# A QKV projection: x transposed by VectorE in 32x32 blocks instead of by TensorE, float32r operands instead of bf16, w in column chunks

## The chip, the cores and the metric

The kernel runs on one core of one Trainium2 chip. The metric is the device time of that core in microseconds (us). Lower is better. Times are medians of a few executions. The profile describes one execution, and its span is some 1 to 2 us shorter than the time of the same execution.

## The reference

```python
x: (16, 512, 768) float32, w_qkv: (768, 2304) float32     # standard normal
qkv = np.matmul(x, w_qkv)
return np.stack([q, k, v], axis=0)                         # q, k, v: the three 768-column parts
```

Seen as one matrix product it is 8192 x 768 times 768 x 2304. With 128 rows of x to a tile there are 64 tiles. In both kernels a matmul contracts over the partitions, 128 at a time (the 128*128 in the groups of instructions below), so 768 gives six steps, and x is handed to TensorE transposed: 128 values of the contraction index on the partitions, 128 rows along the free axis. A tile takes 24 matmuls with 512 columns of w and 6 matmuls with 256 columns.

## The kernel before

x arrives in its own layout, ScalarE rounds it to bf16, and TensorE transposes it in six 128x128 pieces (matmuls against an identity). Those pieces go to PSUM, and VectorE or ScalarE copies them back to SBUF. The transposes of the next tile are woven between the matmuls of the present one. w is loaded in six row blocks of 128 full rows.

```python
w_bf = wb_pool.tile([P, KT, N3], bf16)
# ... pools: x 2 buffers, xT 3, opsum 7 banks, o 3
for ko in range(KT):                                   # w: 128 partitions, whole rows
    w_scr = w_pool.tile([P, N3], fp32)
    nc.gpsimd.dma_start(w_scr[:], w_qkv[bass.ts(ko, P), :])
    nc.vector.tensor_copy(out=w_bf[:, ko, :], in_=w_scr[:])
# ... emit_tps: one PE transpose; after the sixth, a copy PSUM -> xT
for mi in range(MT):
    # ... load x of tile mi+1, round it to bf16 on ScalarE
    for noff, nsz in n_offs:                           # 512, 512, 512, 512, 256
        ops = opsum_pool.tile([P, 512], fp32, tag="o")
        for ko in range(KT):
            nc.tensor.matmul(ops[:, :nsz], xT[:, ko, :], w_bf[:, ko, noff:noff + nsz],
                             start=(ko == 0), stop=(ko == KT - 1))
            if have_next and ko < 2 and tps_cnt < KT:
                emit_tps(nx_mb, nxT, tps_cnt, use_scalar=(nmi % 2 == 0))
                tps_cnt += 1
        nc.vector.tensor_copy(out=o_sb[:, noff:noff + nsz], in_=ops[:, :nsz])
    # ... three stores, one each to q, k, v
```

## Time and profile before

| | before |
|---|---|
| time, median (lowest to highest) | 419.2 us (419.08 to 419.31) |
| span of the profiled execution | 418.5 us |
| mean granted TensorE clock | 1.00 |
| TensorE busy | 95% |

From the page of the kernel before: busy time of each engine, then TensorE's busy share and its granted clock in tenths over 40 equal slices (9 stands for 90% or more), and the shares of the chain of waits that ended last.

```profile
PE 397.3 (95%) x2260; PEld 210.9 (50%) x2304; DVE 224.6 (54%) x358; ACT 77.7 (19%) x97; POOL 4.0 (1%) x12
...
PE   0589999999999999999999999999999999999996
...
PEclk9999999999999999999999999999999999999999
...
PE 92%; DMA 5%; issue 1%; POOL 1%; DVE 1%; POOLq 0%
```

TensorE bounds this kernel. After the third slice (about 31 us) it never pauses, at full clock, and the chain is TensorE nearly from end to end.

Groups of instructions of the kernel before, with the shapes kept apart. The columns are: line, engine, operation, output and input, count; then busy us and mean ns of one; then the engine's idle time before them and what ended it.

```profile
L113 PE MATMUL ops<-w_bf,nxT 128*128 128x512 bf16 x1468 | 353.4, 380 | 1.4
L113 PEld LDWEIGHTS <-nxT 128*128 128x128 bf16 x1890 | 177.5, 98 | 168.2 <-DVE nxT L88 0.7 <-issue 0.3
L123 DVE COPY o_sb<-ops 128x512 f32<-128x512 f32 x256 | 176.5, 691 | 171.3 <-PE ops L113 171.1
L75 PE MATMUL tps<-id_sb,nx_mb 128*128 128x128 bf16 x378 | 81.9, 223 | 5.5 <-ACT nxT L86 4.5
```

A matmul's "mean ns" is not the spacing of two matmuls: one of 512 columns is listed with 380 ns, yet in the stream they start 0.216 us apart (0.109 at 256 columns, 0.055 to 0.056 for a transpose). The cost is the spacing of their starts: 24 x 0.216 + 6 x 0.109 + 6 x 0.0555 = 6.17 us, the period of a tile seen below. (Some matmul records are missing: 2304 matmuls run, and the page lists 2260.) The transposes take the stream of TensorE for 64 x 6 x 0.055 = 21 us. That is what the change wants to save.

Pieces of the chain of waits of the kernel before, in order of time: start, length, what.

```profile
4.39 22.29 DMA w_scr<-in_w_qkv_dram
...
28.11 8.26 PE ops L113 x41
...
42.11 3.03 PE ops L113 x17
48.28 3.03 PE ops L113 x17
```

The same piece of work comes back every 6.17 us: one tile. 64 x 6.17 = 395 us, and the last matmul ends near 414.8, so all of the start-up is worth 19.9 us of lost TensorE time. The rest, 3.7 us, is the tail.

Stretches of the kernel before: the stretch and its length, busy us of each engine (instructions), granted clock, DMA share, GB/s.

```profile
core 0: us, PE busy (x) PEld busy (x) DVE busy (x) ACT busy (x) POOL busy (x), PEclk, DMA share, GB/s
5.00:10.00 5.00, 0.48 (x5) 0.22 (x3) 0.98 (x1) 1.17 (x2) 0.00 (x0) 1.00 1.01 417
10.00:20.00 10.00, 5.04 (x26) 2.77 (x27) 3.79 (x5) 2.76 (x4) 0.00 (x0) 1.00 1.01 422
```

The loads of the start run at 420 GB/s (417 and 422 in the two stretches).

### The profile page before, as it was taken

The page shows a single profiled execution, that of the slowest core. Times are in us where ns is not written, and L with a number is a line of the kernel's source. Part 1 is how long each engine was busy: PE and PEld are TensorE (multiplying, and loading weights), DVE is VectorE, ACT ScalarE, POOL GpSimd, SP SyncE. Part 2 cuts the span into 40 slices and gives each one's busy share as a digit, 9 for nine tenths or more (in the row PEclk, how much of TensorE's full clock was granted, in tenths as well). Part 3 has the DMA queues.
Part 4 walks back from the last instruction along what each step waited for, and adds up shares of the span by engine and source line. Part 5 has one row for each costly group of instructions (what it writes and reads, how often), then busy time and mean ns, then how long its engine had stood idle before and what let it go on. Part 6 is the DMA issues. An engine that isn't in the chain of part 4 may idle for free.

```text
span 418.5 us, 5827 instructions
## 1 busy us (share of the span) xinstructions
PE 397.3 (95%) x2260; PEld 210.9 (50%) x2304; DVE 224.6 (54%) x358; ACT 77.7 (19%) x97; POOL 4.0 (1%) x12
## 2 busy tenths in 40 slices
PE   0589999999999999999999999999999999999996
PEld 0245555555555555555555555555555555555553
DVE  1456555555555455555555555545555555555554
ACT  3210221221122122022112112212212221221200
POOL 3000000000000000000000000000000000000000
PEclk9999999999999999999999999999999999999999
DMA  8968777778877767877777787787777767778444
GB/s 323 423 258 314 236 257 261 223 272 261 286 219 261 268 226 283 269 246 252 256 241 258 259 285 233 256 262 231 279 263 254 248 253 245 254 267 283 197 184 194
DMA packets 37756, 108.13 MB, mean 258 GB/s; under 512 B 4192, under 2 KB 4192, under 8 KB 36960
## 3 DMA queue, kind: packets, MB, share of 16 engines
q1 hardware_dynamic: 36864, 100.68, 69.7%
q0 software_dynamic: 864, 7.08, 4.1%
q8 instruction: 18, 0.29, 0.3%
q14 instruction: 10, 0.08, 0.1%
HBM read 32.24 MB, written 75.50 MB: 257 GB/s over the span
## 4 chain that ended last, share of the span: by engine, by line
PE 92%; DMA 5%; issue 1%; POOL 1%; DVE 1%; POOLq 0%
PE ops L113 86%; PE tps L75 6%; DMA w_scr<-in_w_qkv_dram 5%; POOL w_scr L66 1%; DVE w_bf L67 0%; DVE o_sb L123 0%; POOLq L151 0%; POOL id_sb masks.py:199 0%; POOL id_sb masks.py:197 0%; POOLq masks.py:199 0%; POOLq L140 0%
## 5 line engine op out<-in xcount | busy, mean ns | idle before, releaser
L113 PE MATMUL ops<-w_bf,nxT 128*128 128x512 bf16 (+1 forms) x1846 | 385.5, 358 | 1.4
L123 DVE COPY o_sb<-ops 128x512 f32<-128x512 f32 (+1 forms) x320 | 201.1, 638 | 171.3 <-PE ops L113 171.1
L113 PEld LDWEIGHTS <-nxT 128*128 128x128 bf16 x1890 | 177.5, 98 | 168.2 <-DVE nxT L88 0.7
L75 PE MATMUL tps<-id_sb,nx_mb 128*128 128x128 bf16 x378 | 81.9, 223 | 5.5 <-ACT nxT L86 4.5
L104 ACT ACTIVATE nx_mb<-nx_m 128x768 bf16<-128x768 f32 x63 | 52.9, 839 | 152.7 <-issue 135.6
L86 ACT ACTIVATE nxT<-tps 128x768 bf16<-128x768 bf16 x31 | 25.2, 811 | 167.9 <-PE tps L75 167.9
L75 PEld LDWEIGHTS <-nx_mb 128*128 128x128 bf16 x378 | 37.4, 100 | 20.9 <-ACT nx_mb L104 4.4
L88 DVE COPY nxT<-tps 128x768 bf16<-128x768 bf16 x32 | 17.8, 557 | 2.2 <-PE tps L75 2.2
L67 DVE CAST w_bf<-w_scr 128x2304 bf16<-128x2304 f32 x6 | 8.2, 1358 | 17.2 <-DMA w_scr<-in_w_qkv_dram 17.2
L113 PE MATMUL ops<-w_bf,xT 128*128 128x512 bf16 (+1 forms) x30 | 9.4, 435 | 6.0 <-DVE w_bf L67 6.0
L113 PEld LDWEIGHTS <-xT 128*128 128x128 bf16 x30 | 3.4, 116 | 9.9 <-ACT xT L86 5.2
L75 PE MATMUL tps<-id_sb,x_mb 128*128 128x128 bf16 x6 | 0.8, 310 | 4.7 <-ACT x_mb L62 4.7
L66 POOL DMA_DIRECT2D w_scr<-in_w_qkv_dram x6 | 3.3, 556 | 0.3 <-issue 0.3
L75 PEld LDWEIGHTS <-x_mb 128*128 128x128 bf16 x6 | 0.6, 138 | 4.7 <-ACT x_mb L62 4.7
L62 ACT ACT_TABLE_LOAD x1 | 1.3, 1283 | 0.7 <-PEq L140 0.7
L62 ACT ACTIVATE x_mb<-x_m 128x768 bf16<-128x768 f32 x1 | 0.8, 842 | 1.7 <-DMA x_m<-in_x_dram 1.7
L86 ACT ACTIVATE xT<-tps 128x768 bf16<-128x768 bf16 x1 | 0.8, 792 | 0.0
masks.py:199 POOL TENSOR_SCALAR_AFFINE_SELECT id_sb<-id_sb 128x128 bf16<-128x128 bf16 x1 | 0.3, 307 | 0.1
masks.py:197 POOL MEMSET id_sb<- 128x128 bf16 x1 | 0.2, 205 | 0.3 <-POOLq L140 0.3
L140 POOL MEMSET const-bfloat16-1.0<- 128x1 bf16 x1 | 0.1, 103 | 0.0
L140 POOL MEMSET const-uint8-127<- 128x1 uint8 x1 | 0.1, 103 | 0.0
L140 POOL MEMSET const-float32-0.0<- 128x1 f32 x1 | 0.1, 100 | 0.2 <-issue 0.2
(1 smaller groups left out, 0.1 us busy)
## 6 DMA issues: line engine op xcount, KB each, us to landing
out_dram<-o_sb SPq DMA_DIRECT2D x192, 384.0 KB, 3.6
nx_m<-in_x_dram SPq DMA_DIRECT2D x63, 384.0 KB, 3.6
w_scr<-in_w_qkv_dram POOLq DMA_DIRECT2D x6, 1152.0 KB, 14.8
x_m<-in_x_dram SPq DMA_DIRECT2D x1, 384.0 KB, 3.0
```

What stands on the lines that cost most here:

```text
L62: nc.scalar.activation(x_mb0[:], x_m0[:], mybir.ActivationFunctionType.Identity)
L66: nc.gpsimd.dma_start(w_scr[:], w_qkv[bass.ts(ko, P), :])
L67: nc.vector.tensor_copy(out=w_bf[:, ko, :], in_=w_scr[:])
L75: nc.tensor.matmul(tps[:, bass.ts(ko, P)], xb_tile[:, bass.ts(ko, P)], id_sb[:], is_transpose=True, start=(ko == 0), stop=(ko == KT - 1),)
L86: nc.scalar.activation(xT_view[:], tps[:], mybir.ActivationFunctionType.Identity)
L88: nc.vector.tensor_copy(out=xT_view[:], in_=tps[:])
L104: nc.scalar.activation(nx_mb[:], nx_m[:], mybir.ActivationFunctionType.Identity)
L113: nc.tensor.matmul(ops[:, :nsz], xT[:, ko, :], w_bf[:, ko, noff:noff + nsz], start=(ko == 0), stop=(ko == KT - 1),)
L123: nc.vector.tensor_copy(out=o_sb[:, noff:noff + nsz], in_=ops[:, :nsz])
L140: nc = _bacc.Bacc("TRN2", target_bir_lowering=False, num_devices=1)
```

## The change

The intent is to take the transposes off TensorE. x is loaded so that each 32-partition group holds one quarter of the contraction index (192 of 768 columns). A 32x32 block transpose on VectorE then yields the layout that the matmuls read, ScalarE writes it again as float32r (fp32r in the listings; called a rounding below), and TensorE runs the product matmuls alone. w is loaded in the matching order, in column chunks (256, then four of 512), so that the first five tiles can start chunk by chunk. ScalarE takes two of the five PSUM evictions of a tile from VectorE. The diff, cut to its core:

```diff
+    mm_dt = mybir.dt.float32r
+    n_offs = [(0, 256)] + [(256 + 512 * i, 512) for i in range(4)]
     # ... pools: x 2 (of four tiles each), xf 3, xT 7, ps 8 banks, o 6
-    for ko in range(KT):
-        w_scr = w_pool.tile([P, N3], fp32)
-        nc.gpsimd.dma_start(w_scr[:], w_qkv[bass.ts(ko, P), :])
-        nc.vector.tensor_copy(out=w_bf[:, ko, :], in_=w_scr[:])
+    def load_w(c):
+        off, sz = n_offs[c]
+        st = ws_pool.tile([P, KT, 512], fp32, name="wst")
+        for i in range(4):
+            nc.scalar.dma_start(
+                st[i * G:(i + 1) * G, :, :sz],
+                w_qkv[i * KC:(i + 1) * KC, off:off + sz].rearrange("(j a) n -> a j n", a=G),
+            )
+        for j in range(0, KT, 2):
+            nc.vector.tensor_copy(out=w_sb[c][:, j:j + 2, :], in_=st[:, j:j + 2, :sz])
+    def load_x(mi, count):
+        t = x_pool.tile([P, 4, 4, KC], fp32, name="xin")
+        rows = x_flat[mi * P:(mi + count) * P, :].rearrange("(g b) k -> b g k", b=G)
+        for i in range(4):
+            dst = t[i * G:(i + 1) * G, :count].rearrange("p t g k -> p (t g) k")
+            nc.sync.dma_start(dst, rows[:, :, i * KC:(i + 1) * KC])
-    # ... emit_tps: TensorE transposes and the copies of their PSUM tile
+    def prep(mi):
+        t, n = xs.pop(mi)
+        xf = xb_pool.tile([P, KT, P], fp32, name="xf")
+        nc.vector.transpose(xf.rearrange("p j (g b) -> p g j b", b=G),
+                            t[:, n].rearrange("p g (j a) -> p g j a", a=G))
+        xt = xT_pool.tile([P, KT, P], mm_dt, name="xt")
+        nc.scalar.activation(xt[:], xf[:], copy)
+        xT[mi] = xt
+    # ... mm: six matmuls of one tile and chunk, then the eviction on VectorE or ScalarE
+    # ... first phase: w chunks 0 to 4, in each the tiles 0 to 4
+    for mi in range(FIRST, MT):
+        if loaded - mi <= 3 and loaded < MT:
+            n = min(4, MT - loaded)
+            load_x(loaded, n)
+            loaded += n
+        if mi + 1 < MT:
+            prep(mi + 1)
+        o_sb = o_pool.tile([P, N3], fp32, name="o")
+        order = range(5) if mi < MT - 1 else (1, 2, 3, 4, 0)
+        for c in order:
+            mm(mi, c, o_sb, c % 2 == 0)
+        store(mi, o_sb)
```

More of the change, by code (lines that the diff above doesn't have):

```diff
@@ L4 @@
 import concourse.tile as tile
-from concourse import bass_utils, mybir
-from concourse.masks import make_identity
+from concourse import mybir
 from concourse._compat import with_exitstack
@@ L19 @@
     P = 128
+    G = 32
     B, T, H = x.shape
@@ L23 @@
     N3 = w_qkv.shape[1]
-    assert N3 == 3 * H
-    assert K % P == 0 and M % P == 0
     KT = K // P
+    KC = K // 4
     MT = M // P
+    fp32 = mybir.dt.float32
+    mm_dt = mybir.dt.float32r
+    copy = mybir.ActivationFunctionType.Identity
     x_flat = x.rearrange("b t h -> (b t) h")
     out_flat = out.rearrange("s b t h -> s (b t) h")
-    n_offs = []
-    o = 0
-    while o < N3:
-        sz = min(512, N3 - o)
-        n_offs.append((o, sz))
-        o += sz
-    bf16 = mybir.dt.bfloat16
@@ L42 @@
-    fp32 = mybir.dt.float32
-    id_pool = ctx.enter_context(tc.tile_pool(name="id", bufs=1))
-    id_sb = id_pool.tile([P, P], bf16)
-    make_identity(nc, id_sb)
-    w_pool = ctx.enter_context(tc.tile_pool(name="w", bufs=6))
+    n_offs = [(0, 256)] + [(256 + 512 * i, 512) for i in range(4)]
+    ws_pool = ctx.enter_context(tc.tile_pool(name="ws", bufs=2))
     wb_pool = ctx.enter_context(tc.tile_pool(name="wb", bufs=1))
-    w_bf = wb_pool.tile([P, KT, N3], bf16)
     x_pool = ctx.enter_context(tc.tile_pool(name="x", bufs=2))
-    xb_pool = ctx.enter_context(tc.tile_pool(name="xb", bufs=2))
@@ L54 @@
-    xT_pool = ctx.enter_context(tc.tile_pool(name="xT", bufs=3))
-    tpsum_pool = ctx.enter_context(tc.tile_pool(name="tpsum", bufs=1, space=bass.MemoryType.PSUM))
-    opsum_pool = ctx.enter_context(tc.tile_pool(name="opsum", bufs=7, space=bass.MemoryType.PSUM))
-    o_pool = ctx.enter_context(tc.tile_pool(name="o", bufs=3))
-    x_m0 = x_pool.tile([P, K], fp32, tag="x")
-    nc.sync.dma_start(x_m0[:], x_flat[bass.ts(0, P), :])
-    x_mb0 = xb_pool.tile([P, K], bf16, tag="xb")
-    nc.scalar.activation(x_mb0[:], x_m0[:], mybir.ActivationFunctionType.Identity)
@@ L64 @@
-    for ko in range(KT):
-        w_scr = w_pool.tile([P, N3], fp32)
-        nc.gpsimd.dma_start(w_scr[:], w_qkv[bass.ts(ko, P), :])
-        nc.vector.tensor_copy(out=w_bf[:, ko, :], in_=w_scr[:])
-    tps_state = {}
-    def emit_tps(xb_tile, xT_tile, ko, use_scalar):
-        if ko == 0:
-            tps_state['t'] = tpsum_pool.tile([P, KT * P], bf16, tag="t", name="tps")
-        tps = tps_state['t']
-        nc.tensor.matmul(
-            tps[:, bass.ts(ko, P)],
-            xb_tile[:, bass.ts(ko, P)],
-            id_sb[:],
-            is_transpose=True,
-            start=(ko == 0),
-            stop=(ko == KT - 1),
-        )
-        if ko == KT - 1:
-            xT_view = xT_tile.rearrange("p k m -> p (k m)")
-            if use_scalar:
-                nc.scalar.activation(xT_view[:], tps[:], mybir.ActivationFunctionType.Identity)
-            else:
-                nc.vector.tensor_copy(out=xT_view[:], in_=tps[:])
@@ L90 @@
-    xT_tiles = {}
-    xT0 = xT_pool.tile([P, KT, P], bf16, tag="xt")
-    xT_tiles[0] = xT0
-    for ko in range(KT):
-        emit_tps(x_mb0, xT0, ko, use_scalar=True)
-    for mi in range(MT):
-        xT = xT_tiles.pop(mi)
-        nmi = mi + 1
-        have_next = nmi < MT
-        if have_next:
-            nx_m = x_pool.tile([P, K], fp32, tag="x")
-            nc.sync.dma_start(nx_m[:], x_flat[bass.ts(nmi, P), :])
-            nx_mb = xb_pool.tile([P, K], bf16, tag="xb")
-            nc.scalar.activation(nx_mb[:], nx_m[:], mybir.ActivationFunctionType.Identity)
-            nxT = xT_pool.tile([P, KT, P], bf16, tag="xt")
-            xT_tiles[nmi] = nxT
-        tps_cnt = 0
-        o_sb = o_pool.tile([P, N3], fp32)
-        for noff, nsz in n_offs:
-            ops = opsum_pool.tile([P, 512], fp32, tag="o")
-            for ko in range(KT):
-                nc.tensor.matmul(
-                    ops[:, :nsz],
-                    xT[:, ko, :],
-                    w_bf[:, ko, noff:noff + nsz],
-                    start=(ko == 0),
-                    stop=(ko == KT - 1),
-                )
-                if have_next and ko < 2 and tps_cnt < KT:
-                    emit_tps(nx_mb, nxT, tps_cnt, use_scalar=(nmi % 2 == 0))
-                    tps_cnt += 1
-            nc.vector.tensor_copy(out=o_sb[:, noff:noff + nsz], in_=ops[:, :nsz])
@@ new lines @@
+    xb_pool = ctx.enter_context(tc.tile_pool(name="xb", bufs=3))
+    xT_pool = ctx.enter_context(tc.tile_pool(name="xT", bufs=7))
+    ps_pool = ctx.enter_context(tc.tile_pool(name="ps", bufs=8, space=bass.MemoryType.PSUM))
+    o_pool = ctx.enter_context(tc.tile_pool(name="o", bufs=6))
+    w_sb = [wb_pool.tile([P, KT, sz], mm_dt, name=f"w{c}") for c, (_, sz) in enumerate(n_offs)]
+    def load_w(c):
[8 more added lines that the diff above has]
+            nc.vector.tensor_copy(out=w_sb[c][:, j:j + 2, :], in_=st[:, j:j + 2, :sz])
@@ new lines @@
+    xs = {}
+    def load_x(mi, count):
[4 more added lines that the diff above has]
+            nc.sync.dma_start(dst, rows[:, :, i * KC:(i + 1) * KC])
+        for n in range(count):
+            xs[mi + n] = (t, n)
+    xT = {}
+    def prep(mi):
+        t, n = xs.pop(mi)
+        xf = xb_pool.tile([P, KT, P], fp32, name="xf")
+        nc.vector.transpose(
+            xf.rearrange("p j (g b) -> p g j b", b=G),
+            t[:, n].rearrange("p g (j a) -> p g j a", a=G),
+        )
+        xt = xT_pool.tile([P, KT, P], mm_dt, name="xt")
+        nc.scalar.activation(xt[:], xf[:], copy)
+        xT[mi] = xt
@@ L124, with mm, store @@
+    def mm(mi, c, o_sb, evac):
+        off, sz = n_offs[c]
+        ps = ps_pool.tile([P, 512], fp32, name="ps")
+        for j in range(KT):
+            nc.tensor.matmul(ps[:, :sz], xT[mi][:, j, :], w_sb[c][:, j, :], start=(j == 0), stop=(j == KT - 1))
+        if evac:
+            nc.vector.tensor_copy(out=o_sb[:, off:off + sz], in_=ps[:, :sz])
+        else:
+            nc.scalar.activation(o_sb[:, off:off + sz], ps[:, :sz], copy)
+    def store(mi, o_sb, parts=3):
         for s in range(3):
@@ L125 @@
             nc.sync.dma_start(out_flat[s, bass.ts(mi, P), :], o_sb[:, bass.ts(s, H)])
+    FIRST = 5
+    load_x(0, 1)
+    load_w(0)
+    load_x(1, 4)
+    prep(0)
+    for c in range(1, 5):
+        load_w(c)
+    for mi in range(1, FIRST):
+        prep(mi)
+    load_x(FIRST, 4)
+    loaded = FIRST + 4
+    o_first = [o_pool.tile([P, N3], fp32, name="o") for _ in range(FIRST)]
+    for c in range(5):
+        for mi in range(FIRST):
+            mm(mi, c, o_first[mi], (mi + c) % 2 == 0)
+            if c == 4:
+                store(mi, o_first[mi])
@@ L129 @@
+    prep(FIRST)
+    for mi in range(FIRST, MT):
[10 more added lines that the diff above has]
+        store(mi, o_sb)
 _INS = ['x', 'w_qkv']
```

## The prediction

> **What bounds the kernel now.** TensorE. The page's first part shows it 95% busy, and the chain of waits puts 92% of the span on it (86% product matmuls, 6% transposes). The timeline shows matmuls starting every 0.216 us (512 columns), about 0.11 us (256) and 0.055 us (128, the transposes). One 128-row tile is therefore 24 x 0.216 + 6 x 0.11 + 6 x 0.055 = 6.17 us, which is the period seen between pieces of the chain; 64 tiles make 395 us. The last matmul ends near 414 us, so start-up costs about 19 us of TensorE time (it runs without gaps only from 28 us, when the last row block of w has been cast). The tail is 4 us. VectorE is 54% busy, ScalarE 19%, DMA about 0.76 in the steady part (stretches table), 1.01 at 420 GB/s during the first 20 us.
>
> **What the change does.**
> 1. Removes the 384 PE transposes and their PSUM copies: 64 x 6 x 0.055 = -21 us on the critical path.
> 2. Product matmuls stay 1920 in number and the same in shape, but float32r, and each loads its own weights. [...] Loads took 98 ns in the trace with bf16; if slower they can still hide under 0.216 us, less surely under 0.11 us. No run here shows either yet. This is the largest risk: an unhidden 98 ns load would add 1920 x 0.098 = 188 us.
> 3. VectorE gains 64 transposes of 128x768 fp32. From the two evictions (512: 691 ns, 256: 424 ns) I estimate 0.96 us each. It loses two of five evictions to ScalarE: per tile 0.96 + 0.42 + 2 x 0.69 = 2.8 us of a 5.84 us period. ScalarE: 0.84 + 2 x about 0.6 = 2.0 us. Neither binds. Bursts of four transposes (about 4 us) fit into eight PSUM banks (over 8 us of TensorE work).
> 4. x comes in 768-byte runs instead of 3 KB. DMA work now is about 4.7 us per tile, a quarter of it x; even 1.5 times for x gives 5.3 us, under 5.84 but close.
> 5. Start-up. w in column chunks should let TensorE start early, but the order of instructions shows that ScalarE issues all w loads, waiting for VectorE to free staging buffers, before it rounds tiles 1 to 4; and the fourth tile's transpose stands behind the third 512-column chunk's casts. At 420 GB/s about 9 MB must land first (21 us plus latency, cast, transpose, rounding): TensorE runs on from about 27 us, with only the 3.3 us of chunk 0 done. Effective start-up about 24 us, 5 us worse than before.
>
> **Sum.** 64 x 5.84 = 374, plus 24 start-up, [...]plus 4 tail: 403 us. Range 391 to 455, long upwards because of point 2. Chances: faster 0.60, within 2% 0.18, slower 0.22.
>
> **What would show it.** Matmul spacing of 0.216 us at 512 columns and 5.84 us per tile; no transposes on TensorE; VectorE transposes near 0.96 us; gapless TensorE from 25 to 28 us; DMA share near 0.85 in the steady part and never the releaser of TensorE.
>
> **What would make it wrong.** Matmul spacing above 0.22 us (weight loads exposed[...]); VectorE transposes several times 0.96 us, stalling evictions; the DMA queues saturating on 768-byte packets; or start-up overlapping better than the order suggests (then nearer 393).

The sum came to 403 us. Passages that no trace or run of this case shows are cut from the text above, and with them one term of the sum, of about 1 us; the terms that are left make 374 + 24 + 4 = 402. That float32r keeps the bf16 spacing of 0.216 and 0.11 us, on which the 374 rests, was the author's assumption: the trace had shown it for bf16 alone. That a weight load can lie under a matmul is seen in the kernel before (loads busy 210.9 us in all, beside a TensorE that is busy 95% of the span). The 0.6 us of an eviction on ScalarE was an estimate for which the text names no numbers.

## The result, and the profile after

| | before | after |
|---|---|---|
| time, median | 419.25 us (4 runs) | 494.8 us (4 runs: 489.06, 496.15, 497.9, 493.45) |
| ratio of the fast runs, 95% interval | | 1.175 (1.167 to 1.182) |
| span of the profiled execution | 418.5 us | 487.3 us |
| mean granted TensorE clock | 1.00 | 0.975 |
| TensorE busy | 95% | 85% |

A ratio here is the mean time of one kernel's fast runs over that of the other's fast runs of the same rounds, so it is not quite the ratio of the medians quoted beside it. The 497.9 us run counts as slow by the 1.5% rule and is left out of the ratio; the three fast runs have a mean of 492.9 us, and later differences are taken from it. The change is 17% slower; the prediction was 403 us, and 494.8 lies far above its range.

The same parts of the page, for the changed kernel:

```profile
PE 412.1 (85%) x1920; PEld 343.6 (71%) x1920; DVE 177.6 (36%) x269; ACT 130.2 (27%) x195; POOL 0.2 (0%) x4
...
PE   0105999999997979799897979899797997979796
...
PEclk9999999999999999999999999989899998989989
...
PE 83%; DMA 8%; DVE 3%; ACT 2%; issue 2%; SPq 0%; DVEq 0%
```

Three things are new. TensorE is idle almost through the first three slices (37 us; before, through one). Then it drops to 70 or 80% again and again. Late in the run the granted clock drops too (the 8s).

The groups of the changed kernel:

```profile
L87 PE MATMUL ps<-w,xt 128*128 128x512 f32 x1536 | 368.1, 397 | 0.0
L87 PEld LDWEIGHTS ps<-w,xt 128*128 128x128 f32 x1920 | 343.6, 195 | 139.3 <-ACT xt L80 63.9 <-issue 12.7
L91 ACT ACTIVATE o<-ps 128x512 f32<-128x512 f32 x128 | 76.2, 597 | 275.6 <-PE ps L87 268.3 <-DVE xf L75 2.9 <-DMA out_dram<-o 2.9
...
L75 DVE STREAM_TRANSPOSE xf<-xin 128x768 f32<-128x768 f32 x64 | 57.3, 946 | 8.8 <-DMA xin<-in_x_dram 8.8
L80 ACT ACTIVATE xt<-xf 128x768 fp32r<-128x768 f32 x64 | 53.4, 843 | 71.0 <-DVE xf L75 39.2 <-DMA wst<-in_w_qkv_dram 30.6 <-PE ps L87 0.8
```

The new operations cost what the prediction said: 946 ns for a block transpose (estimate 0.96 us), 597 ns for an eviction on ScalarE (0.6), 843 ns for a rounding (0.84). The TensorE transposes are gone. A weight load takes 195 ns instead of 98. And VectorE waited for x only 8.8 us in the whole run.

**Start.** The stretches of the start, in the columns shown above, for the changed kernel:

```profile
5.00:10.00 5.00, 0.00 (x0) 0.00 (x0) 0.98 (x1) 1.97 (x2) 0.00 (x0) 1.00 1.12 218
10.00:20.00 10.00, 1.62 (x6) 1.35 (x6) 4.22 (x7) 0.00 (x0) 0.00 (x0) 1.00 1.12 215
...
100.00:200.00 100.00, 94.91 (x459) 79.56 (x458) 37.34 (x58) 28.00 (x43) 0.00 (x0) 1.00 0.74 234
```

The DMA engines look full (share 1.12), yet move only 215 to 218 GB/s, half of the 420 before. Every load of x and w in the changed kernel writes 32 partitions, and those of the kernel before wrote 128. The runs of x are shorter too (768 bytes instead of 3 KB), so this trace alone does not say which of the two halves the rate; e3, e5 and e6 below ask that.

**Gaps.** Pieces of the chain of waits of the changed kernel:

```profile
33.01 9.11 DMA wst<-in_w_qkv_dram
...
44.13 0.90 DVE xf L75
...
45.06 0.85 ACT xt L80
...
45.95 102.38 PE ps L87 x486
...
148.96 0.98 DVE xf L75
...
149.96 0.85 ACT xt L80
...
150.86 25.00 PE ps L87 x120
...
178.39 25.00 PE ps L87 x120
...
288.51 26.64 PE ps L87 x120
```

From 150.86 on TensorE works off four tiles (x120 = 4 x 30 matmuls), stops, works off four, and so on, twelve stops in all. The chain passes through one VectorE transpose and one ScalarE rounding at each stop. The timeline around one such stop (start, length, engine, line, operation; in brackets the idle time before it and what ended it):

```profile
203.41 0.69 DVE L89 COPY o<-ps 128x512 f32<-128x512 f32 x1 [2.03 <-PE ps L87]
...
204.02 3.55 DVE L75 STREAM_TRANSPOSE xf<-xin 128x768 f32<-128x768 f32 x4
...
205.02 3.42 ACT L80 ACTIVATE xt<-xf 128x768 fp32r<-128x768 f32 x4 [2.37 <-DVE xf L75]
...
205.91 10.36 PE L87 MATMUL ps<-w,xt 128*128 128x256 f32 x50 [2.54 <-ACT xt L80]
```

VectorE had been idle for 2.03 us, waiting for TensorE to finish the last PSUM bank of the tile. It copies it out, and only then transposes the next four tiles. TensorE, which has just finished that bank, has no transposed x left: it waits for the copy, the first transpose (0.98 us), and the rounding (0.85 us), 2.54 us in all. VectorE could have transposed during its 2.03 us of idleness, since the x of these tiles had landed: its four loads were issued from 185.97 to 187.77 us, and by the DMA packets of the trace the last of it landed near 195.5 us, 8.5 us before. At the twelve stops it had been there for 8.3 to 10.6 us. VectorE did not start because the copy stands ahead of the transposes in its program. The order of VectorE's instructions around such a group, as the build lists it (there are no times in it; the notes behind # are mine):

```
TensorCopy o<-ps 128x256            # tile n
TensorCopy o<-ps 128x512 x2         # tile n: each waits for TensorE to fill its bank
StreamTranspose xf<-xin x4          # tiles n+1, n+2, n+3, n+4
TensorCopy o<-ps 128x256            # tile n+1
TensorCopy o<-ps 128x512 x2         # tile n+1
```

In the source, `prep(mi + 1)` is written ahead of the matmuls of tile `mi`, but the build placed the group of four behind them. Let a transpose have "no lead" when it stands behind the last VectorE copy of the tile before its own. Among the 59 tiles after the first five, 12 have no lead in this build: the twelve stops. That list needs no chip, and I had it when I predicted.

**Matmul spacing.** VectorE copies out the banks of chunks 0, 2 and 4 of a tile, so its copy starts show TensorE's pace. Three of them from the undisturbed part of the changed kernel:

```profile
154.62 0.69 DVE L89 COPY o<-ps 128x512 f32<-128x512 f32 x1 [1.80 <-PE ps L87]
...
157.34 1.14 DVE L89 COPY o<-ps 128x512 f32<-128x512 f32 x2 [2.03 <-PE ps L87]
...
160.80 0.69 DVE L89 COPY o<-ps 128x512 f32<-128x512 f32 x1 [2.32 <-PE ps L87]
```

Between chunk 2 and chunk 4 lie 12 matmuls of 512 columns: 2.72 / 12 = 0.2267 us each. From chunk 2 to chunk 2 of the next tile lie 30 matmuls: 6.18 us. So a 256-column matmul takes (6.18 - 24 x 0.2267) / 6 = 0.123 us in effect. (The matmul starts themselves lie 0.227 us apart at 512 columns and 0.120 at 256; the first five of 512 behind the six of 256 come 0.229 to 0.236 us apart, and the 0.123 contains that.) The tile takes 6.18 us, where 5.84 had been predicted. That is the 6.17 us of the kernel before: all that the removed transposes gave is lost again in slower matmuls.

**Clock.** The stretch just behind two of the stops, in the columns shown before:

```profile
150.90:154.30 3.40, 3.40 (x18) 2.95 (x19) 1.92 (x3) 2.95 (x4) 0.00 (x0) 1.00 0.00 1
...
288.50:291.90 3.40, 3.38 (x14) 2.86 (x15) 1.97 (x3) 2.86 (x4) 0.00 (x0) 0.72 0.04 10
```

Behind the stop at 288.5 the mean clock of the stretch is 0.72: the records show half clock in a window of 3.41 us that this stretch only partly covers. It starts fewer matmuls, and the four tiles then take 26.64 us instead of 25.00. Seven of the twelve stops are followed by such a window (the last seven), each lengthening the four-tile period from 27.53 to about 29.0 us.

Why the last seven and not the first five? In this trace the clock changes only on a grid of 3.41 us. Two windows of that grid, each with the larger part of a stop in it:

```profile
259.29:262.70 3.41, 1.72 (x10) 1.58 (x11) 3.41 (x5) 2.58 (x4) 0.00 (x0) 1.00 0.37 147
...
286.60:290.01 3.41, 1.50 (x9) 1.39 (x10) 3.41 (x5) 2.36 (x3) 0.00 (x0) 1.00 0.46 177
```

In the first, TensorE is idle for 1.69 us, and full clock follows; in the second it is idle for 1.91 us, and the next window, 290.01 to 293.43, is the one at half clock. At the first five stops no window held more than 1.75 us of idleness, at the last seven one always held 1.91 us or more. The early period of 27.53 us is 8.07 windows, so each stop lay 0.22 us later against the grid than the one before, until one window held 1.91 us of it. In e10 a window with 1.86 us passed as well, and e1 has an exception: there a window with 2.20 us of idleness was followed by full clock. So these are the figures of these runs; a fixed border between them is not shown.

The sum, beside the prediction's (spans; the effective start is the time of TensorE's unbroken work less the 24 small matmuls it had done before):

| term | predicted | measured | from |
|---|---|---|---|
| matmuls, 64 tiles | 374 | 395.5 | 64 x 6.18 |
| start-up | 24 | 43.0 | 45.95 - 24 x 0.123 |
| a term from the prediction | 1 | | |
| stops of TensorE | 0 | 33.7 | 12 x (27.53 - 4 x 6.18), about 2.8 each |
| half clock | 0 | 10.5 | 7 x about 1.5 |
| tail | 4 | 4.2 | 487.3 less 483.1, the end of the last matmul |
| sum | 403 | 486.9 | span 487.3 |

Against the kernel before, the 69 us are: start-up +23, matmuls +0.6, stops +34, half clock +10.5, tail +0.5.

### The profile page after: what moved, and what is told of

Same layout as the page of the kernel before. It is cut to its first block, busy times and chain, and to the rows that moved or that the text cites. A ratio compares the mean times of both kernels' runs of the same rounds, so it can differ in the third digit from the quotient of the medians.

```text
span 487.3 us, 5081 instructions
## 1 busy us (share of the span) xinstructions
PE 412.1 (85%) x1920; PEld 343.6 (71%) x1920; DVE 177.6 (36%) x269; ACT 130.2 (27%) x195; POOL 0.2 (0%) x4
## 4 chain that ended last, share of the span: by engine, by line
PE 83%; DMA 8%; DVE 3%; ACT 2%; issue 2%; SPq 0%; DVEq 0%
PE ps L87 83%; DMA xin<-in_x_dram 6%; DVE xf L75 3%; ACT xt L80 2%; DMA wst<-in_w_qkv_dram 2%; DVE o L89 0%; DVE w L57 0%; SPq L66 0%; DVEq L75 0%; DVEq L57 0%; DVEq L89 0%
## 5 line engine op out<-in xcount | busy, mean ns | idle before, releaser
L87 PE MATMUL ps<-w,xt 128*128 128x512 f32 (+1 forms) x1920 | 412.1, 377 | 71.0 <-ACT xt L80 58.3
L87 PEld LDWEIGHTS ps<-w,xt 128*128 128x128 f32 x1920 | 343.6, 195 | 139.3 <-ACT xt L80 63.9
L89 DVE COPY o<-ps 128x512 f32<-128x512 f32 (+1 forms) x190 | 114.1, 602 | 270.1 <-PE ps L87 269.0
L91 ACT ACTIVATE o<-ps 128x512 f32<-128x512 f32 (+1 forms) x130 | 76.9, 593 | 275.6 <-PE ps L87 268.3
L80 ACT ACTIVATE xt<-xf 128x768 fp32r<-128x768 f32 x64 | 53.4, 843 | 71.0 <-DVE xf L75 39.2
L75 DVE STREAM_TRANSPOSE xf<-xin 128x768 f32<-128x768 f32 x64 | 57.3, 946 | 8.8 <-DMA xin<-in_x_dram 8.8
L57 DVE CAST w<-wst 128x1024 fp32r<-128x1024 f32 (+1 forms) x15 | 8.7, 635 | 27.0 <-DMA wst<-in_w_qkv_dram 27.0
```

Of the source, the lines that this page charges most:

```text
L57: nc.vector.tensor_copy(out=w_sb[c][:, j:j + 2, :], in_=st[:, j:j + 2, :sz])
L75: nc.vector.transpose(xf.rearrange("p j (g b) -> p g j b", b=G), t[:, n].rearrange("p g (j a) -> p g j a", a=G),)
L80: nc.scalar.activation(xt[:], xf[:], copy)
L87: nc.tensor.matmul(ps[:, :sz], xT[mi][:, j, :], w_sb[c][:, j, :], start=(j == 0), stop=(j == KT - 1))
L89: nc.vector.tensor_copy(out=o_sb[:, off:off + sz], in_=ps[:, :sz])
L91: nc.scalar.activation(o_sb[:, off:off + sz], ps[:, :sz], copy)
```

## The experiments

The theory after this reading has three independent parts. (1) float32r matmuls are themselves spaced wider than bf16 ones. (2) The stops come from the order of VectorE's instructions, and the half clock follows the stops (before the first four runs I still counted the clock as a loss of its own that would go with float32r, as the expectation of e1 shows). (3) The start is slow because transfers to 32 partitions run at half rate (215 to 218 GB/s, against 417 to 422 to 128 partitions in the kernel before). The rivals were: for (1) that the clock or the weight-load stream, not the type, sets the pace everywhere; for (2) that x arrives late, or that float32r's own demand lowers the clock; for (3) that the 768-byte runs of x, or the place of the w loads in ScalarE's program, are what is slow. Twelve kernels ran, on four chips (e1 to e4, e5 to e8, e9 to e11, e12), each beside the kernel before on the same chip (medians 419.3 to 420.4 us). Medians of all runs, and ratios of the fast runs to the kernel before. Of e3 and e5 only one run in four was fast (488.5 and 516.8 us), and they have no ratio; the medians of these two are those of slow runs:

| run | what | us | ratio (95%) | clock of the profiled run | transposes without lead, as built |
|---|---|---|---|---|---|
| changed kernel | | 494.8 | 1.175 (1.167 to 1.182) | 0.975 | 12 |
| e1_bf16 | bf16 operands | 471.1 | 1.121 (1.117 to 1.125) | 0.967 | 12 |
| e2_x_early | x loaded earlier | 454.8 | 1.083 (1.079 to 1.087) | 0.997 | 0 |
| e3_x_rows | 3 KB runs of x (wrong result) | 497.3 | | 0.968 | 12 |
| e4_w_pool | w issued by GpSimd | 486.4 | 1.156 (1.149 to 1.163) | 0.979 | 9 |
| e5_w128 | w to 128 partitions | 525.6 | | 0.93 | 14 |
| e6_all128 | w and x to 128 (wrong result) | 433.9 | 1.034 (1.032 to 1.036) | 0.993 | 0 |
| e7_bf16_x_early | bf16 and x earlier | 433.2 | 1.032 (1.030 to 1.034) | 0.993 | 0 |
| e8_best | e7 and w to 128 | 412.9 | 0.983 (0.981 to 0.986) | 0.989 | 2 |
| e9_384 | e2 with six chunks of 384 | 457.1 (1 run) | | 1.00 | 0 |
| e10_best2 | e8, more lead and buffers | 413.5 | 0.986 (0.983 to 0.989) | 0.997 | 1 |
| e11_best_fp32r | e8 with float32r | 437.1 | 1.040 (1.035 to 1.044) | 0.986 | 2 |
| e12_best3 | e10, loads reordered | 411.9 | 0.981 (0.979 to 0.983) | 0.990 | 0 |

### e1_bf16

```diff
-    mm_dt = mybir.dt.float32r
+    mm_dt = mybir.dt.bfloat16
```

> Only the matmul operand type goes from float32r to bfloat16 (x and w are still loaded, transposed and ordered as in the changed kernel). Theory A (the loss against the prediction is four separate terms: slower float32r matmuls +26 us, lower granted clock +10 us, twelve gaps of 2.5 us +30 us, late start +18 us): spacing returns to 0.216/0.11 us, clock to 1.00, the twelve gaps and the start near 43-46 us stay: about 450 us. Rival B (the gaps are x arriving late): a faster TensorE only waits longer, groups of four tiles keep their 27.5 us period, about 480 us.

Measured: 471.1 us, result correct, 22 us below the changed kernel (470.9 against 492.9, fast runs). Two of VectorE's evictions of e1_bf16, again the chunk-2 copies of two tiles with the chunk-4 copy between them:

```profile
156.36 0.69 DVE L89 COPY o<-ps 128x512 f32<-128x512 f32 x1 [2.17 <-PE ps L87]
158.95 1.08 DVE L89 COPY o<-ps 128x512 f32<-128x512 f32 x2 [1.90 <-PE ps L87]
...
162.20 0.69 DVE L89 COPY o<-ps 128x512 f32<-128x512 f32 x1 [2.16 <-PE ps L87]
```

The spacing is 2.59 / 12 = 0.216 us, the tile takes 5.84 us, and a 256-column matmul (5.84 - 24 x 0.2158) / 6 = 0.11 us: the numbers that the prediction had assumed for float32r. So float32r costs about 11 ns more per matmul (0.227 against 0.216 us, 0.120 against 0.109), 0.34 us per tile with what follows the small ones, 22 us in 64 tiles. The stops and the half clock stay (twelve stops, nine windows, mean clock 0.967), so they do not come from the type. The 450 us of theory A are missed by 21 us, and the 480 us of rival B as well: the half clock that theory A took away with the type is still there (nine windows, some 13 us, estimated at 1.5 us each), and a stop costs more than its 2.5 us of idleness (about 2.8 us in the table above). One more thing in my reckoning before this run was mis-sized: I had read the 256-column spacing as 0.135 us off pieces of the chain, whose length contains the whole listed time of one matmul (277 ns or more in the changed kernel); the eviction starts give 0.123, the matmul starts 0.120.

### e2_x_early

```diff
-    x_pool = ctx.enter_context(tc.tile_pool(name="x", bufs=2))
+    x_pool = ctx.enter_context(tc.tile_pool(name="x", bufs=3))
...
-        if loaded - mi <= 3 and loaded < MT:
+        if loaded - mi <= 7 and loaded < MT:
```

> float32r kept; a third x buffer, and each x load emitted four tiles earlier, so that the build puts the four transposes ahead of the last evictions of the tile before. Theory A (gaps are the place of the transposes in VectorE's order): the 2.5 us gaps vanish, -30 us, about 457 us at the same clock; the start does not improve. Rival B (x lands late because 768-byte packets fill the queues): gaps stay in number or size, 480 us or more. If the clock depends on how busy TensorE is, it falls below 0.94 and gives part of the gain back.

Measured: 454.8 us, correct, 38 us below the changed kernel's fast runs. The build now places no transpose without lead (0 of 59 instead of 12). The chain of waits of e2_x_early, from the end of the start-up, is one piece:

```profile
53.25 394.74 PE ps L87 x1890
```

1890 matmuls without a stop, and no half clock from 60 to 400 us (1.00 in every stretch there; mean of the run 0.997). This is the decisive run for the gaps: operations, sizes and type are as in the changed kernel, and both losses are gone together. It was bought with a later start, 53.25 instead of 45.95 us, because the additional x loads share the slow start with w (by 42 us, by the DMA packets, 4.2 MB of x and 5.1 MB of w had landed, against 3.5 and 5.8 MB in the changed kernel). Note what the edit did: it loads x earlier and it moves the transposes, so this run alone does not tell rival B from theory A. The trace of the changed kernel does: x had been there 8.3 to 10.6 us before each stop. Loading it earlier changed where the build put the transposes; that is what TensorE had waited for.

### e3_x_rows

```diff
-        rows = x_flat[mi * P:(mi + count) * P, :].rearrange("(g b) k -> b g k", b=G)
+        rows = x_flat[mi * P:(mi + count) * P, :].rearrange("(t p) k -> p t k", p=P)
...
-            dst = t[i * G:(i + 1) * G, :count].rearrange("p t g k -> p (t g) k")
-            nc.sync.dma_start(dst, rows[:, :, i * KC:(i + 1) * KC])
+            dst = t[i * G:(i + 1) * G, :count].rearrange("p t g k -> p t (g k)")
+            nc.sync.dma_start(dst, rows[i * G:(i + 1) * G])
```

> Wrong result on purpose: x is loaded by as many DMAs of the same size onto the same 32 partitions each, but in 3 KB runs (whole rows) instead of 768-byte runs; everything else and every engine's order the same. Theory C (short runs halve the read rate at the start): 5 to 20 us moves about 400 GB/s instead of 215, TensorE runs on from about 30 us instead of 46, about -16 us, gaps stay. Rival D (32-partition transfers, or w's 2 KB runs, are the limit): rate at the start and the time stay within 4 us.

This loads whole rows (3 KB runs) to the same 32 partitions each; the result is wrong. Measured: 497.3 us (488.53 at best), no gain. Its start, as a stretch:

```profile
10.00:20.00 10.00, 1.62 (x6) 1.35 (x6) 4.22 (x7) 0.00 (x0) 0.00 (x0) 1.00 1.06 216
```

216 GB/s, as before the edit (215). The length of the runs is not what makes the start slow. (The profiled run counted as slow, for its half clock later on, 0.94 to 0.98 in the stretches from 100 us; the stretch shown is listed with 1.00.)

### e4_w_pool

```diff
-            nc.scalar.dma_start(
+            nc.gpsimd.dma_start(
```

> w loads issued by GpSimd instead of ScalarE, so that the rounding of tiles 1 to 4 no longer stands behind w's staging waits. Theory E (ScalarE's order makes the late start): chunk 0 of tiles 1 to 4 runs near 20 us and TensorE has done about 17 us of work by 44 us: -14 us at the start. The build also moves the steady transposes ahead of one or two evictions, so some of the 2.5 us gaps should shrink too: 445 to 472 us. Rival C (only the read rate sets the start): the start gains under 4 us.

Measured: 486.4 us, correct; theory E's 445 to 472 us are missed. TensorE runs without pause from 69.75 us, with 120 matmuls (24.1 us) done before: on the scale of the table above a start-up of about 45.7 us (43.0 in the changed kernel), so taking the w loads away from ScalarE brought the start nothing. What gain there is, 7 us against the fast runs, fits the stops: nine instead of twelve in the build, and six half-clock windows (mean clock 0.979), two of them in the start (0.94 from 30 to 60 us, 0.96 from 60 to 100). ScalarE's order, which my prediction saw rightly in the program, is not what sets the length of the start.

### e5_w128

```diff
-        for i in range(4):
-            nc.scalar.dma_start(st[i * G:(i + 1) * G, :, :sz], ...)      # cut
+        wv = w_qkv.rearrange("(p j) n -> p j n", j=KT)
+        for j in range(0, KT, 2):
+            nc.scalar.dma_start(st[:, j:j + 2, :sz], wv[:, j:j + 2, off:off + sz])
...
-            t[:, n].rearrange("p g (j a) -> p g j a", a=G),
+            t[:, n].rearrange("p g (a j) -> p g j a", a=G),
```

> The changed kernel with w loaded by DMAs over all 128 partitions (K is dealt to partitions so that partition p holds w rows 6p to 6p+5; the transposes read x with a step of 6, the result stays right). x keeps its 32-partition, 768-byte loads. Theory F (a transfer onto 32 partitions moves at half rate, about 215 GB/s, whatever its run length): the 5.5 MB of w ahead of the gapless start move at about 420 GB/s, which saves about 12 us: TensorE gapless from about 34 us instead of 46, time about 12 us below the changed kernel. Rival G (one hardware queue per issuing engine, or 1 to 2 KB runs, limit the start): still about 215 GB/s, no gain over 4 us. The 2.5 us gaps stay in both.

w now goes to all 128 partitions, with the contraction index dealt out as p x 6 + j; to match, the transpose reads x with a step of six elements. The result is correct. The loads between 10 and 20 us rose to 304 GB/s, and TensorE ran without pause from 42.16 us instead of 45.95. But the time was 516.8 us in the one fast run (525.5 to 525.9 in the three slow ones), 24 us worse than the changed kernel's fast runs, where I had expected it 12 better. The group of e5_w128's transposes shows why:

```profile
L73 DVE STREAM_TRANSPOSE xf<-xin 128x768 f32<-128x768 f32 x64 | 95.7, 1550 | 0.0
```

The transpose takes 1550 ns with this read pattern, against 946. It stands in each stop, so the stops grew from about 2.5 to 3.1 us (fourteen of them), and the half clock with them: twelve windows, nine of them twice as long (6.83 us), 71.7 us at half clock in all (the mean clock of 0.93 over 515.0 us). At those nine, the stop left about 2.0 us of idleness in one window of the clock's grid and 1.1 in the next. This miss was useful: it shows how much a stop costs once it lasts a little longer.

### e6_all128

```diff
     # as e5_w128, and:
-        for i in range(4):
-            dst = t[i * G:(i + 1) * G, :count].rearrange("p t g k -> p (t g) k")
-            nc.sync.dma_start(dst, rows[:, :, i * KC:(i + 1) * KC])
+        for n in range(count):
+            nc.sync.dma_start(t[:, n].rearrange("p g k -> p (g k)"), x_flat[bass.ts(mi + n, P), :])
```

> Wrong result on purpose: as e5_w128, and x too by 128-partition DMAs of the same 384 KB each (whole 3 KB rows). Theory F: about 400 GB/s from 5 us on, TensorE gapless from about 27 us, 18 us or so below the changed kernel; and each steady group of x loads lands in clearly under 6 us. Rival G: rate stays near 215 GB/s. With e3_x_rows (3 KB runs on 32 partitions, no gain) this separates the number of partitions from the run length.

x goes to all 128 partitions too, which the block transpose cannot put right, so the result is wrong (relative error 1.23). The start of e6_all128:

```profile
10.00:20.00 10.00, 0.71 (x2) 0.42 (x2) 6.87 (x8) 0.00 (x0) 0.00 (x0) 1.00 1.04 393
```

393 GB/s, and TensorE without pause from 32.13 us, 13.8 us earlier. With e3 (216 GB/s with 3 KB runs to 32 partitions) and e4 this settles the start: not run length, not ScalarE's order, but 32 partitions against 128. Each x tile is one DMA here, the transposes come singly in the build (none without lead), and there are no stops: 433.9 us, 59 us below the changed kernel's fast runs where 18 or so had been expected from the start alone.

### e7_bf16_x_early

> bfloat16 operands and the early x loads of e2_x_early together. Theory A with the clock following the gaps: no 2.5 us gaps, so no half-clock windows: clock 1.00 from 60 us on, 5.84 us per tile, start near 50 us as in e2: 374 + 50 + 4 = 428 us, 26 us below e2_x_early, although bfloat16 alone gained about 20 us or less. Rival H (the lower clock comes from the steady power of VectorE, ScalarE and DMA work, or time): clock about 0.95 again after 200 us, 440 us or more.

The edits of e1 and e2 together. Measured: 433.2 us, correct; 428 had been expected. No stops, clock 0.993; from 100 to 300 us it is 1.00, so rival H (a lower clock from the steady work) fails. Beside e2 (454.8 us), which differs in the type alone and has the same order of transposes, float32r costs 21.6 us: the 22 us of the spacings, in a kernel whose stops and clock are not mixed in. The start is still the slow one (TensorE runs from 53.03 us, 50.4 on the scale of the table), as expected; the 5 us that I had missed are elsewhere: a tail of 5.8 us instead of 4, one half-clock window right behind the start (about 1.5 us), and the 1.7 us by which the time exceeds the span.

### e8_best

The edits of e7, with the w layout of e5 issued from `nc.sync`.

> All remedies: bfloat16 operands, x loads early, w on 128 partitions, and every load issued by the sync engine in the order of use, so that ScalarE waits for no w buffer. Theory: 374 us of matmuls at 5.84 us per tile, start-up of 20 to 28 us, 4 us tail: 398 to 406 us, faster than both kernels. If a gap-free TensorE at 5.84 us a tile is limited by DMA (1.57 MB a tile, x on 32 partitions), the time stays above 412 us and the waits name x or the stores.

Measured: 412.9 us, correct, ratio 0.983 (0.981 to 0.986): 1.7% faster than the kernel before, inside the 2% band that counts as the same. TensorE starts in earnest at 24.8 us. It is not the expected 398 to 406, because the build has two transposes without lead here, and both cost: stops of 3.3 us (51.3 to 54.65) and 3.1 us (79.8 to 82.9), with two half-clock windows. The second one shows a new wait, on the output stores, which the expectation had named for a DMA limit (above 412 us, waits that name the stores): from 60 to 100 us the DMA share is 1.00. From the chain of waits of e8_best:

```profile
70.70 9.80 DMA out_dram<-o
80.50 1.51 DVE xf L73
82.04 0.85 ACT xt L78
```

After that it goes at 5.84 us a tile to the end, with a DMA share of 0.87 from 100 to 200 us, so DMA does not bind the steady part.

### e9_384

```diff
     # e2_x_early, and:
-    n_offs = [(0, 256)] + [(256 + 512 * i, 512) for i in range(4)]
+    n_offs = [(384 * i, 384) for i in range(6)]
```

> float32r, early x loads as in e2_x_early, but w cut into six chunks of 384 columns instead of one of 256 and four of 512 (36 matmuls per tile instead of 30). It asks what the float32r matmul costs over its columns: measured so far 0.2267 us at 512 and 0.135 us at 256 (bfloat16 0.216 and 0.11). Theory J (a fixed extra of about 13 ns per matmul, and a floor of 0.135 us set by the weight load that binds only at 256): 384/512 of 213.3 plus 13.4 = 0.173 us, 6.24 us per tile. Rival K (the extra falls in a straight line with columns): 0.181 us, 6.51 us per tile.

This asks what the extra time of float32r depends on. Two evictions of e9_384 on VectorE with 12 matmuls of 384 columns between them:

```profile
204.69 0.56 DVE L89 COPY o<-ps 128x384 f32<-128x384 f32 x1 [1.52 <-PE ps L87]
206.78 0.56 DVE L89 COPY o<-ps 128x384 f32<-128x384 f32 x1 [1.52 <-PE ps L87]
```

2.09 / 12 = 0.174 us; over nine such intervals the mean is 0.1733, which makes 6.24 us per tile (36 matmuls). The bf16 line through 0.109 at 256 and 0.2158 at 512 gives an estimate of 0.162 at 384, so the extra is about 11 ns here too: the same at 256, 384 and 512 columns, and not a share of the column count (0.181 had been the rival's number). A floor of 0.135 at 256 columns, which my text had assumed, is not there (the matmul starts of the changed kernel lie 0.120 us apart). What the fixed 11 ns are, I have not settled: the weight loads are longer as well (189 to 195 ns against 98), but no run separated the two.

### e10_best2

```diff
     # e8_best, and:
-    o_pool = ... bufs=6
+    o_pool = ... bufs=9
-            nc.sync.dma_start(dst, ...)
+            (nc.sync if mi < 9 else nc.gpsimd).dma_start(dst, ...)
     # the first phase stores each third of the output as soon as it is complete
-            prep(mi + 1)
+            prep(mi + 2)
```

> e8_best with nine output buffers, the first five tiles' thirds stored as soon as they are complete, transposes two tiles ahead, and the steady x loads issued by GpSimd so that they do not stand behind stores in the sync engine's queue. Theory (e8_best still lost about 10 us to waits for output buffers between 50 and 83 us and to two half-clock windows): those go, start-up about 21 us stays: 398 to 405 us. Rival (DMA is the bound there: 1.00 share from 60 to 100 us): waits move elsewhere, 408 us or more.

Measured: 413.5 us, correct. One stop is left (at 59 us; it is split into 1.86 and 1.24 us over two windows of the clock's grid, and no half clock follows), then TensorE runs 343.8 us in one piece; but it starts only at 31.19 us (24.82 in e8), since an x load now issued by GpSimd joins the start and one x transfer takes 16.78 us (10.80 in e8). What was won at the stops was lost at the start, as the rival of the expectation had it (408 us or more).

### e11_best_fp32r

```diff
     # e8_best, and:
-    mm_dt = mybir.dt.bfloat16
+    mm_dt = mybir.dt.float32r
```

> e8_best with float32r operands again, one line differs. Theory A: 6.25 us per tile instead of 5.84 adds 26 us less what e8_best lost to full DMA queues (about 8 us), so 430 to 440 us: slower than the kernel before even with every other loss mended. If float32r costs nothing but the order and the loads did, it stays under 419 us.

Measured: 437.1 us, correct, 4.0% slower than the kernel before, 24 us above e8_best. With the start and all but two stops mended, float32r alone still turns the change into a loss.

### e12_best3

```diff
     # e10_best2, and: the first four tiles are prepared before the w chunks; the x loads of
     # tiles 5 to 8 go just ahead of the last w chunk, those of tiles 9 to 12 just behind it;
     # tiles 5 and 6 are prepared before the first phase; x comes from nc.sync below tile 13
```

> e10_best2 with the first two steady x loads put back on the sync engine, one of them between the third and fourth 512-column chunk of w, and the next tiles' transposes emitted before the first phase. In e10_best2 an early x load on 32 partitions competed with tiles 1 to 4 and w, and one transpose still stood behind the last eviction of the tile before; the build now shows none that does. Theory (what is left is start-up alone): 374 us at 5.84 us per tile, TensorE gapless from about 25 us with 2.6 us of work done, 4 us tail: 399 to 404 us. Rival (DMA is the bound between 40 and 100 us): new waits for output buffers or x, 408 us or more.

Measured: 411.9 us, correct, ratio 0.981 (0.979 to 0.983). Not the expected 399 to 404 us. TensorE starts early, then waits 5.7 us for the last w chunk, which stands behind an x load of 13.8 us; its first cast also stands behind two block transposes on VectorE (2.97 us) that waited for that x, the same kind of order as at the stops. It then runs 6.8 us at half clock. Its median is the lowest, but its interval overlaps that of e8; whether it passes 2% is unclear.

## Why the prediction was wrong, point by point

What it had right: TensorE bounds the kernel before; 21 us of transposes leave it; VectorE, ScalarE and their new operations cost what was estimated, and neither is busy beyond half; the DMA share of the steady part (0.74 at the changed kernel's pace, 0.82 to 0.85 at the 5.84 us pace of e7) never holds TensorE up; the chances of wider matmul spacing were named as a risk.

Where it was wrong, in order of size, 84 us in the sum:

1. **"Bursts of four transposes (about 4 us) fit into eight PSUM banks (over 8 us of TensorE work)."** This step failed, and it cost 44 us of the 84: 34 in stops, 10.5 in half clock behind them. It asks whether transposes delay the evictions. The harm came the other way round: an eviction that waits for TensorE stands ahead of the transposes that TensorE will need next. The number of stops (12) could be counted in the built program; e2 loaded x earlier, which moved the transposes ahead of those evictions, and both losses went. That x was not late before, the landings show (8.3 to 10.6 us ahead of each stop).
2. **"Matmul spacing of 0.216 us at 512 columns and 5.84 us per tile."** This was the author's assumption for float32r, from a trace of bf16. The spacing stayed near it, but the size was off: 0.2267 and 0.123 us, 6.18 us per tile, 22 us in 1920 matmuls. The text gave a threshold for it (above 0.22 us) and then let the sum run on the lower value. e1, e7 against e2, and e11 against e8 each give 22 to 24 us.
3. **"At 420 GB/s about 9 MB must land first."** The order of events in the start was right: the fourth tile's transpose behind the casts of the third large chunk, at 44.13 us. The rate was half of it, 215 to 218 GB/s, because all transfers now write 32 partitions each (e3: 216 with 3 KB runs to 32; e6: 393 to 128). Start-up was 43 us instead of 24. The 420 GB/s came from a profile in which w went to 128 partitions; a rate read there does not hold for another layout.

The spread of the changed kernel's runs (489 to 498 us) belongs to the clock. Their spans were 487.3, 494.3, 496.1 and 491.7 us at mean clocks of 0.975, 0.959, 0.959 and 0.965. Span times (1 - clock) gives 12.2, 20.3, 20.3 and 17.2 us, and the spans less these are 475.1, 474.0, 475.8 and 474.5: equal within 2 us. By these figures the profiled run lost seven windows of 3.41 us at half clock (7 x 1.7 = 12 us), and the two runs at 20.3 us about twelve, one for each stop (an estimate): the same stops fell differently on the clock's grid.

What stays open: where the 11 ns of a float32r matmul come from. Why the build puts a group of transposes behind the evictions is not shown either, only that it does, and that earlier loads move them; and no run changed that order while it left the x loads as they were.

## What to carry to other kernels

When work leaves the bounding engine for another one, look in the built order for what stands ahead of it there. VectorE kept to that order here (idle for 2.03 us beside x that had landed 8.5 us before), so the wait for the bounding engine held that engine's next input behind it (2.54 us of TensorE a stop). A transfer rate belongs to a layout (here 215 GB/s to 32 partitions, 393 to 128), so read it again when the number of partitions per transfer changes. And a stop of 2.5 us cost more than 2.5 us when the clock dropped after it (about 1.5 us more for a window of 3.41 us at half clock); whether it did depended here on how the stop fell on the clock's 3.41 us windows, so a dozen short stops deserve the same care as one long one.
